# Up projections of a SwiGLU feed-forward: four grid tiles as one moving operand of 512 columns

## The chip, the core and the metric

The kernel runs on one core of a Trainium2 chip. The metric is the device time of one launch in microseconds (us); the median of three runs of the kernel before is 1928.17 us (1925.45 to 1930.57). The core has five engines that run side by side and each work through their own instructions in a fixed order: PE (TensorE: matrix products, with a separate stream of weight loads, PEld), DVE (VectorE), ACT (ScalarE), POOL (GpSimd) and SP (SyncE, here only an issuer of transfers). They wait for each other through semaphores. Matrix products are written to PSUM, which has eight banks of 128 x 512 floats.

## What is computed

A trunk of two layers over 512 latent tokens on a grid (64 wide) and 256 context tokens, with a model width of 1024. Each layer is a modulated RMSNorm, one input projection, four token mixers, an output projection with a gated residual, and then the part that matters here: a second modulated RMSNorm and a SwiGLU of hidden width 2816 with a gated residual. In the last layer the context tokens are left out of everything behind the mixers.

```
def swiglu(h, w1, w3, w2):
    return (jax.nn.silu(h @ w1) * (h @ w3)) @ w2

    for l in range(DEPTH):
        ...
        hx = rms_norm(x, norm2_g[l]) * (1.0 + scx2) + shx2
        x = x + gx2 * swiglu(hx, ffn_w1[l], ffn_w3[l], ffn_w2[l])
        if l < DEPTH - 1:
            ...
            y = y + gy2 * swiglu(hy, ffn_w1[l], ffn_w3[l], ffn_w2[l])
    return rms_norm(x, final_norm_g)
```

## The kernel before

Tokens lie in tiles of 128: tiles 0 to 3 are the grid, tiles 4 and 5 the context. Two tiles make a pair p: p = 0 and 1 for the grid, p = 2 for the context. Every large product is done with both operands split into a rounded high part and the remainder as a low part; `mm3` (L465 to L469) issues three matmuls for it, high by high (L467), high by low (L468) and low by high (L469).

The normed tokens of the second norm are made in `norm_T` (L490): per pair it transposes on PE, scales and shifts on DVE, rounds the high part on ACT (L508) and subtracts for the low part (`sub_lo`, L213). The two results of a pair are tiles of the tag `b8`, [128, 8, 256]: eight blocks k of the model width, 256 tokens each. They stay in SBUF for the whole feed-forward as `h2[p]`.

The feed-forward runs over 11 groups g of 256 hidden units. A group has

- the weights: w1 and w3 in two units of [128, 4, 256] each, w2 in two units of [128, 1024]; each is loaded into a `raw` tile (issued from ACT's queue, four buffers), rounded into `wh` on ACT (L449, five buffers) and subtracted into `wl` on DVE or POOL (L213);
- the up projections, `ffn_up(W, p)` (L1457): for both halves j of the hidden units 24 matmuls (eight k by three) into one PSUM tile `ps`, with the weights as stationary operand and 256 tokens of `h2[p]` as moving operand. For w1 ACT takes the silu into `s1` (L1464). For w3 DVE multiplies (L1466), ACT rounds the product into `gh` (L1467) and `sub_lo` puts the remainder into `gl` (L213; every third call of `sub_lo` in the whole kernel goes to POOL, the others to DVE). In the profile `s1` tiles are named P, `gh` and `gl` are named b;
- the down projection (L1490 on): for each token tile t and each half b of the output six matmuls into a PSUM tile `pg`, with `gh` and `gl` as stationary and 512 columns of w2 as moving operand: three for j = 0, three for j = 1. DVE multiplies by the gate (`nat`, L1353), POOL adds to the residual (L1355). Group 9 has no down projection of its own; it is done with group 10's.

Within a group w1 comes first for all pairs and then w3 for all pairs (pairs 2, 0, 1 in layer 0; 0, 1 in layer 1). Group 0 holds the last pair back, since its norm is still being made. In layer 0 the modulation of the next layer is computed beside this, 12 steps a group, two behind each `ffn_up`: each step loads a tile `qT` of `ada_w` (issued from ACT's queue) and multiplies and adds it on DVE (L397); at some steps PE sums over partitions (`pu`, L404) and transposes (L429) behind a copy by ACT (L426).

The text of the program gives the dependences. The order on each engine, and which PSUM bank and buffer a tile gets, are set when the program is built, by a scheduler that models durations; on the chip each engine then keeps that order.

```
                for j in range(2):
                    ps = PS("s")
                    for k in range(8):
                        mm3(ps[:, 0:256], W(k, j), (h2[p][0][:, k], h2[p][1][:, k]), k == 0, k == 7)
```

Of the kernel before, what the change touches and what calls it, by code (L numbers as in the profile page):

```python
# [7 lines left out]
F32R = mybir.dt.float32r  # L8
# [79 lines left out]
def build(tc, I, out, opts=None):  # L88
# [401 lines left out]
    def norm_T(l, which, p, blks, hT, ks, tags=("s",)):  # L490
        s = 0 if p < 2 else 1
        sh, sc = (0, 1) if which == 1 else (2, 3)
        if p not in hT:
            hT[p] = (T("b8", [P, 8, 256], F32R), T("b8", [P, 8, 256], F32R))
        hi, lo = hT[p]
        for i2, k2 in enumerate(ks):
            ps = PS(tags[i2 % len(tags)]).rearrange("p (a b) -> p a b", a=2)
            for k in range(2):
                for i in range(2):
                    pe.transpose(ps[:, k, i * P:(i + 1) * P], blks[i][k2 + k], ident)  # L500
            hf = T(HF, [P, 2, 256])
            for k in range(2):
                a, b = (modT[l][:, s, x, k2 + k:k2 + k + 1] for x in (sc, sh))
                if HFE[k]:
                    act.activation(hf[:, k], ps[:, k], AF.Identity, bias=b, scale=a)
                else:
                    dve.tensor_scalar(hf[:, k], ps[:, k], a, b, op0=ALU.mult, op1=ALU.add)
            act.activation(hi[:, k2:k2 + 2, :], hf, AF.Copy)  # L508
            sub_lo(lo[:, k2:k2 + 2, :], hf, hi[:, k2:k2 + 2, :])

    def norm_pair(l, which, p, hT):
        norm_T(l, which, p, [norm_stats(2 * p), norm_stats(2 * p + 1)], hT, range(0, 8, 2), NT_[which])
# [1 line left out]
    def hs(hT, t, k):  # L514
        hi, lo = hT[t // 2]
        o = (t % 2) * P
        return hi[:, k, o:o + P], lo[:, k, o:o + P]

    ahead = {}

# [283 lines left out]
    for l in range(LAYERS):  # L804
# [635 lines left out]
        for g in range(11):  # L1440
# [14 lines left out]
            W3 = tr_units(v3)  # L1455

            def ffn_up(W, p):  # L1457
                for j in range(2):
                    ps = PS("s")
                    for k in range(8):  # L1460
                        mm3(ps[:, 0:256], W(k, j), (h2[p][0][:, k], h2[p][1][:, k]), k == 0, k == 7)
                    sl = slice(p * 256, (p + 1) * 256)
                    if W is W1:
                        act.activation(s1[j][:, sl], ps[:, 0:256], AF.Silu)  # L1464
                        continue
                    dve.tensor_tensor(s1[j][:, sl], ps[:, 0:256], s1[j][:, sl], op=ALU.mult)  # L1466
                    act.activation(gh[j][:, sl], s1[j][:, sl], AF.Copy)  # L1467
                    sub_lo(gl[j][:, sl], s1[j][:, sl], gh[j][:, sl])

            np_ = ntile // 2  # L1470
            ps_ = [2, 0, 1] if not last else [0, 1]
            early = np_ - 1 if g == 0 else np_
            for W in (W1, W3):
                for p in ps_[:early]:
                    ffn_up(W, p)
                    steps(2)
            for p in ps_[early:]:
                ffn_up(W1, p)
# [47 lines left out]
```

## Time and profile before

| | |
|---|---|
| median of three runs | 1928.17 us (1925.45 to 1930.57) |
| the profiled execution: its time, its span | 1927.69 us, 1925.9 us |
| feed-forward of layer 0: stretch of the span, length | 550.2 to 1149.0, 598.8 us |
| feed-forward of layer 1: stretch of the span, length | 1535.6 to 1902.2, 366.6 us |
| PE busy in these two | 589.91 us and 365.02 us |
| matmuls of the up projections | 5280, each of 256 columns |
| matmuls of the down projections | 792 in layer 0, 528 in layer 1, each of 512 columns |

A span is the time from the first to the last instruction; the run's own time is 1.8 us more. A matmul's duration in the profile contains its way through the array, so that neighbours overlap; how fast PE works is read from the distance between the starts of matmuls that follow each other.

### The profile page before, as it was taken

To read this page: it belongs to the slowest core of one execution; us is meant where nothing else is said; L and a number is where in the kernel's file an instruction comes from. 1 tells how busy PE (TensorE), PEld (TensorE's weight loads), DVE (VectorE), ACT (ScalarE), POOL (GpSimd) and SP (SyncE) were. 2 spreads that over 40 slices of the span, in tenths; PEclk is the share of its full clock that TensorE was granted. 3 is DMA by queue.
4 is the path that set the end of the run, shared out by engine and by line. 5 is a ranking of instruction groups with operands and counts; after the bars stand their busy time and mean duration, and the time that the engine had idled before them with its cause. 6 is when DMAs were issued, how large, how long until landed. Compare 5 with 4: busy or idle time off the path is not lost.

```text
span 1925.9 us, 32215 instructions
## 1 busy us (share of the span) xinstructions
PE 1832.2 (95%) x12367; PEld 1596.9 (83%) x12367; DVE 1196.8 (62%) x2743; ACT 688.9 (36%) x1597; POOL 614.3 (32%) x573
## 2 busy tenths in 40 slices
PE   7899999899999999999999999899889999999997
PEld 3677776778889989999899978678778899999996
DVE  5796886777898776453334283465588854344336
ACT  3325653255542111222122233464255532222223
POOL 0211113223124553444444121111232145636442
PEclk9999999899999999999999999999999999999998
DMA  7665435453124345342222122422434143223321
GB/s 233 209 205 156 139 98 181 133 167 82 61 83 147 111 153 186 110 136 64 62 67 66 54 97 81 119 73 92 138 111 109 34 125 95 88 88 93 105 77 44
DMA packets 193572, 215.48 MB, mean 112 GB/s; under 512 B 66660, under 2 KB 141578, under 8 KB 193418
## 3 DMA queue, kind: packets, MB, share of 16 engines
q10 hardware_dynamic: 75840, 111.17, 18.3%
q1 hardware_dynamic: 117578, 102.25, 18.0%
q8 instruction: 97, 1.59, 0.3%
q14 instruction: 57, 0.47, 0.1%
HBM read 192.76 MB, written 20.63 MB: 111 GB/s over the span
## 4 chain that ended last, share of the span: by engine, by line
PE 65%; DVE 8%; issue 2%; POOL 2%; DMA 1%; ACT 1%; SPq 0%; ACTq 0%; DVEq 0%; POOLq 0%
PE ps L467 10%; PE ps L468 10%; PE ps L469 10%; PE pg L469 8%; PE pg L467 8%; PE pg L468 8%; PE po L592 2%; PE ps L626 2%; PE pt L579 2%; DVE wl L213 1%; DVE nat L1353 1%; DVE PT L397 1%; DVE P L613 1%; DVE b L1239 1%; DMA qT<-in_ada_w_dram 0%
## 5 line engine op out<-in xcount | busy, mean ns | idle before, releaser
L467 PE MATMUL ps<-b,wh 128*128 128x256 f32 x1760 | 501.9, 285 | 3.8 <-ACT P L1464 3.8
L468 PE MATMUL ps<-b,wh 128*128 128x256 f32 x1760 | 500.9, 285 | 0.0
L469 PE MATMUL ps<-b,wl 128*128 128x256 f32 x1760 | 500.3, 284 | 0.4 <-POOL wl L213 0.4
L467 PE MATMUL pg<-wh,b 128*128 128x512 f32 (+2 forms) x1128 | 441.9, 392 | 1.2 <-ACT b L508 0.9
L469 PE MATMUL pg<-wh,b 128*128 128x512 f32 (+2 forms) x1128 | 440.7, 391 | 0.6 <-POOL b L213 0.6
L468 PE MATMUL pg<-wl,b 128*128 128x512 f32 (+2 forms) x1128 | 439.6, 390 | 1.2 <-DVE rs_yn L288 0.6
L467 PEld LDWEIGHTS ps<-b,wh 128*128 128x128 f32 x1760 | 340.1, 193 | 7.1 <-ACT P L1464 4.1
L468 PEld LDWEIGHTS ps<-b,wh 128*128 128x128 f32 x1760 | 340.1, 193 | 0.8
L469 PEld LDWEIGHTS ps<-b,wl 128*128 128x128 f32 x1760 | 340.2, 193 | 0.6 <-POOL wl L213 0.6
L213 DVE TENSOR_TENSOR wl<-raw,wh 128x1024 fp32r<-128x1024 f32 (+1 forms) x130 | 200.8, 1549 | 199.0 <-ACT wh L449 197.8
L449 ACT ACTIVATE wh<-raw 128x1024 fp32r<-128x1024 f32 (+1 forms) x196 | 202.7, 1049 | 256.9 <-PE pg L469 210.4
L1355 POOL TENSOR_TENSOR b<-b,nat 128x512 f32<-128x512 f32 (+1 forms) x204 | 221.3, 1103 | 114.2 <-DVE nat L1353 81.6
L213 POOL TENSOR_TENSOR wl<-raw,wh 128x1024 fp32r<-128x1024 f32 (+1 forms) x66 | 165.9, 2514 | 265.1 <-ACT wh L449 254.3
L467 PEld LDWEIGHTS pg<-wh,b 128*128 128x128 f32 x1128 | 214.4, 190 | 38.9 <-issue 1.7
L469 PEld LDWEIGHTS pg<-wh,b 128*128 128x128 f32 x1128 | 214.2, 190 | 38.9 <-issue 3.9
L468 PEld LDWEIGHTS pg<-wl,b 128*128 128x128 f32 x1128 | 214.1, 190 | 38.1 <-DVE wl L213 1.7
L1353 DVE TENSOR_TENSOR nat<-pg,gate 128x512 f32<-128x512 f32 x240 | 162.0, 686 | 85.6 <-PE pg L469 80.2
L213 POOL TENSOR_TENSOR b<-P,b 128x256 fp32r<-128x256 f32 x36 | 28.9, 804 | 327.3 <-ACT b L1467 327.3
L1467 ACT ACTIVATE b<-P 128x256 fp32r<-128x256 f32 x110 | 45.7, 416 | 233.0 <-DVE P L1466 221.9
L1466 DVE TENSOR_TENSOR P<-ps,P 128x256 f32<-128x256 f32 x110 | 46.4, 422 | 129.6 <-PE ps L469 129.5
L1464 ACT ACTIVATE P<-ps 128x256 f32<-128x256 f32 x110 | 41.5, 383 | 213.4 <-PE ps L469 131.6
L397 DVE SCALAR_TENSOR_TENSOR PT<-qT,consts,PT 128x512 f32<-128x512 f32 x112 | 102.1, 927 | 19.3 <-DMA qT<-in_ada_w_dram 18.4
(322 smaller groups left out, 2446.5 us busy)
## 6 DMA issues: line engine op xcount, KB each, us to landing
raw<-in_ffn_w_dram ACTq DMA_DIRECT2D x132, 512.0 KB
qT<-in_ada_w_dram ACTq DMA_DIRECT2D x96, 256.0 KB
raw<-in_w_in_dram SPq DMA_DIRECT2D x40, 512.0 KB
a<-in_ada_w_dram SPq DMA_DIRECT2D x32, 256.0 KB
a<-in_ada_w_dram ACTq DMA_DIRECT2D x32, 256.0 KB
xn<-in_ada_w_dram ACTq DMA_DIRECT2D x32, 256.0 KB
raw<-in_w_out_dram SPq DMA_DIRECT2D x16, 512.0 KB
ldq<-q_d SPq DMA_DIRECT2D x40, 128.0 KB
```

The lines of the kernel that those rows point to most:

```text
L213: eng.tensor_tensor(out, full, hi.bitcast(F32), op=ALU.subtract)
L397: dve.scalar_tensor_tensor(acc[s], w, sS[:, k, s:s + 1], acc[s], op0=ALU.mult, op1=ALU.add)
L449: act.activation(hi, raw_ap, AF.Copy)
L467: pe.matmul(ps, a[0], b[0], start=first, stop=False)
L468: pe.matmul(ps, a[0], b[1], start=False, stop=False)
L469: pe.matmul(ps, a[1], b[0], start=False, stop=last)
L579: pe.transpose(ps[:, i * P:(i + 1) * P], Pm[:, (b0 + i) * P:(b0 + i + 1) * P], ident)
L1353: dve.tensor_tensor(tm, ps, gates[(0 if t < 4 else 2) + b], op=ALU.mult)
L1355: eng.tensor_tensor(ap, ap, tm[:, a:c], op=ALU.add)
L1464: act.activation(s1[j][:, sl], ps[:, 0:256], AF.Silu)
L1466: dve.tensor_tensor(s1[j][:, sl], ps[:, 0:256], s1[j][:, sl], op=ALU.mult)
L1467: act.activation(gh[j][:, sl], s1[j][:, sl], AF.Copy)
```

## The change

`norm_T` makes, for the second norm's grid pairs, four tiles of [128, 4, 512] instead of two pairs of [128, 8, 256]: two for the high and two for the low part, each with four of the blocks k and the 512 tokens of both pairs. `h2[0]` and `h2[1]` are now views of 256 columns in them, and `h2["x"]` gives all 512 columns of a block. Readers of `hT` call `hi(k)` and `lo(k)` instead of indexing a tile; the first norm's tiles and the context pair keep their form, and the SBUF used is the same.

`ffn_up(W, "x")` does the four grid tiles at once: 24 matmuls of 512 columns into one PSUM tile (a whole bank), then silu, product, rounding and remainder on 512 columns. Group 0 keeps the pairs and their order. The other ten groups of each layer do, for w1 and then for w3, the context pair (layer 0) and "x". The modulation steps come three behind each of the four calls instead of two behind each of the six.

```diff
         if p not in hT:
-            hT[p] = (T("b8", [P, 8, 256], F32R), T("b8", [P, 8, 256], F32R))
+            if which == 2 and p < 2:
+                X = [[T("b8", [P, 4, 512], F32R) for _ in range(2)] for _ in range(2)]
+                hT["x"] = [lambda k, x=x: x[k // 4][:, k % 4] for x in X]
+                for q in range(2):
+                    hT[q] = [lambda k, n=1, x=x, q=q: x[k // 4][:, k % 4:k % 4 + n, 256 * q:256 * q + 256] for x in X]
+            else:
+                X = [T("b8", [P, 8, 256], F32R) for _ in range(2)]
+                hT[p] = [lambda k, n=1, x=x: x[:, k:k + n] for x in X]
...
-            act.activation(hi[:, k2:k2 + 2, :], hf, AF.Copy)
-            sub_lo(lo[:, k2:k2 + 2, :], hf, hi[:, k2:k2 + 2, :])
+            act.activation(hi(k2, 2), hf, AF.Copy)
+            sub_lo(lo(k2, 2), hf, hi(k2, 2))
...
             def ffn_up(W, p):
+
+                sl = slice(0, 512) if p == "x" else slice(p * 256, (p + 1) * 256)
+                n = sl.stop - sl.start
                 for j in range(2):
-                    ps = PS("s")
+                    ps = PS("s")[:, 0:n]
                     for k in range(8):
-                        mm3(ps[:, 0:256], W(k, j), (h2[p][0][:, k], h2[p][1][:, k]), k == 0, k == 7)
-                    sl = slice(p * 256, (p + 1) * 256)
+                        mm3(ps, W(k, j), [x(k) if p == "x" else x(k)[:, 0] for x in h2[p]], k == 0, k == 7)
                     if W is W1:
-                        act.activation(s1[j][:, sl], ps[:, 0:256], AF.Silu)
+                        act.activation(s1[j][:, sl], ps, AF.Silu)
                         continue
-                    dve.tensor_tensor(s1[j][:, sl], ps[:, 0:256], s1[j][:, sl], op=ALU.mult)
+                    dve.tensor_tensor(s1[j][:, sl], ps, s1[j][:, sl], op=ALU.mult)
...
-            for W in (W1, W3):
-                for p in ps_[:early]:
-                    ffn_up(W, p)
-                    steps(2)
-            for p in ps_[early:]:
-                ffn_up(W1, p)
-                ffn_up(W3, p)
+            if g == 0:
+                ps_ = [2, 0, 1] if not last else [0, 1]
+                for W in (W1, W3):
+                    for p in ps_[:-1]:
+                        ffn_up(W, p)
+                        steps(2)
+                for W in (W1, W3):
+                    ffn_up(W, ps_[-1])
+            else:
+                for W in (W1, W3):
+                    for p in ([2, "x"] if not last else ["x"]):
+                        ffn_up(W, p)
+                        steps(3)
```

How the order on PE changes where the up projections of a group end and its down projection begins (here layer 1, group 5): before, the last matmul of the up projections (p = 1, j = 1) and the first nine of the down projection. Of the stationary operands, b_3569 and b_3571 are `gh` and `gl` of j = 0, b_3570 and b_3572 those of j = 1.

```order
L469 MATMUL ps_18892<-b_3315_16918,wl_18701 128x256
L467 MATMUL pg_18932<-wh_18922,b_3569_18676 128x512
L468 MATMUL pg_18932<-wl_18923,b_3569_18676 128x512
L469 MATMUL pg_18932<-wh_18922,b_3571_18678 128x512
L467 MATMUL pg_18932<-wh_18928,b_3570_18677 128x512
L468 MATMUL pg_18932<-wl_18929,b_3570_18677 128x512
L469 MATMUL pg_18932<-wh_18928,b_3572_18679 128x512
L467 MATMUL pg_18942<-wh_18922,b_3569_18676 128x512
L468 MATMUL pg_18942<-wl_18923,b_3569_18676 128x512
L469 MATMUL pg_18942<-wh_18922,b_3571_18678 128x512
```

Each output tile takes its three matmuls of j = 0 and its three of j = 1 at once. The same place on PE now; b_3513 and b_3515 are `gh` and `gl` of j = 0, b_3514 and b_3516 those of j = 1.

```order
L469 MATMUL ps_17272<-b_3248_15695,wl_17189 128x512
L467 MATMUL pg_17312<-wh_17302,b_3513_17164 128x512
L468 MATMUL pg_17312<-wl_17303,b_3513_17164 128x512
L469 MATMUL pg_17312<-wh_17302,b_3515_17166 128x512
L467 MATMUL pg_17322<-wh_17302,b_3513_17164 128x512
L468 MATMUL pg_17322<-wl_17303,b_3513_17164 128x512
L469 MATMUL pg_17322<-wh_17302,b_3515_17166 128x512
L467 MATMUL pg_17333<-wh_17302,b_3513_17164 128x512
L468 MATMUL pg_17333<-wl_17303,b_3513_17164 128x512
L467 MATMUL pg_17312<-wh_17308,b_3514_17165 128x512
L468 MATMUL pg_17312<-wl_17309,b_3514_17165 128x512
L469 MATMUL pg_17312<-wh_17308,b_3516_17167 128x512
```

Eight matmuls of j = 0, taken from three output tiles, now stand between the end of the up projections and the first use of `gh` of j = 1; two more stand before the first use of its `gl`.

On DVE in layer 0, group 1, behind the product of j = 0 of the last call: before (P_6961 is `s1` of j = 1, b_1565 its `gl`, L397 the modulation).

```order
L397 SCALAR_TENSOR_TENSOR PT_7745<-qT_7749,consts,PT_7745 128x512
L397 SCALAR_TENSOR_TENSOR PT_7746<-qT_7749,consts,PT_7746 128x512
L397 SCALAR_TENSOR_TENSOR PT_7745<-qT_7809,consts,PT_7745 128x512
L1466 TENSOR_TENSOR P_6961<-ps_7356,P_6961 128x256
L397 SCALAR_TENSOR_TENSOR PT_7746<-qT_7809,consts,PT_7746 128x512
L213 TENSOR_TENSOR b_1565_6965<-P_6961,b_1563_6963 128x256
L1353 TENSOR_TENSOR nat_7411<-pg_7404,gate_6424 128x512
```

Now:

```order
L397 SCALAR_TENSOR_TENSOR PT_7586<-qT_7653,consts,PT_7586 128x512
L397 SCALAR_TENSOR_TENSOR PT_7585<-qT_7657,consts,PT_7585 128x512
L213 TENSOR_TENSOR wl_7437<-raw_7434,wh_7436 128x1024
L1475 TENSOR_TENSOR P_6961<-ps_7242,P_6961 128x512
L397 SCALAR_TENSOR_TENSOR PT_7586<-qT_7657,consts,PT_7586 128x512
L213 TENSOR_TENSOR wl_7443<-raw_7440,wh_7442 128x1024
```

The product of j = 1 (now L1475) still stands behind modulation steps, two instead of three, and a weight remainder has moved ahead of it; its `gl` has gone to POOL.

## Rows read from the trace of the kernel before

**Rows 1.** Page: busy time of each engine; the chain that ended last.
```profile
PE 1832.2 (95%) x12367; PEld 1596.9 (83%) x12367; DVE 1196.8 (62%) x2743; ACT 688.9 (36%) x1597; POOL 614.3 (32%) x573
PE 65%; DVE 8%; issue 2%; POOL 2%; DMA 1%; ACT 1%; SPq 0%; ACTq 0%; DVEq 0%; POOLq 0%
```
**Rows 2.** Windows: the two feed-forwards; stretch, length, busy time (count), clock, DMA share.
```profile
550.20:1149.00 598.80, 589.91 (x4192) 550.78 (x4190) 346.30 (x553) 142.07 (x252) 239.36 (x215) 0.99 0.33 104
1535.60:1902.20 366.60, 365.02 (x2612) 345.72 (x2611) 163.97 (x245) 106.19 (x172) 176.14 (x146) 1.00 0.29 90
```
**Rows 3.** Timeline of PE, layer 1: start and duration; rows left out are steps alike.
```profile
1626.07 0.28 PE L469 MATMUL ps<-b,wl 128*128 128x256 f32 x1
...
1630.03 0.28 PE L469 MATMUL ps<-b,wl 128*128 128x256 f32 x1
1630.15 0.40 PE L467 MATMUL pg<-wh,b 128*128 128x512 f32 x1
...
1632.22 0.39 PE L467 MATMUL pg<-wh,b 128*128 128x512 f32 x1
...
1640.83 0.39 PE L469 MATMUL pg<-wh,b 128*128 128x512 f32 x1
1641.06 0.28 PE L467 MATMUL ps<-b,wh 128*128 128x256 f32 x1
```
**Rows 4.** Groups by form in the two feed-forwards: count, busy us, mean ns, idle before.
```profile
L467 PE MATMUL ps<-b,wh 128*128 128x256 f32 x1056 | 302.6, 287 | 3.8 <-ACT P L1464 3.8
L467 PE MATMUL ps<-b,wh 128*128 128x256 f32 x704 | 199.3, 283 | 0.0
```
**Rows 5.** Timeline of PE and DVE, layer 1, group 1, around the down projection's start.
```profile
1596.09 0.28 PE L469 MATMUL ps<-b,wl 128*128 128x256 f32 x1
1596.21 0.40 PE L467 MATMUL pg<-wh,b 128*128 128x512 f32 x1
...
1596.41 0.42 DVE L1466 TENSOR_TENSOR P<-ps,P 128x256 f32<-128x256 f32 x1 [1.54 <-PE ps L469]
1596.75 2.17 DVE L213 TENSOR_TENSOR wl<-raw,wh 128x1024 fp32r<-128x1024 f32 x1
1598.85 0.41 DVE L213 TENSOR_TENSOR b<-P,b 128x256 fp32r<-128x256 f32 x1
...
1596.87 0.42 ACT L1467 ACTIVATE b<-P 128x256 fp32r<-128x256 f32 x1 [0.56 <-DVE P L1466]
```
**Rows 6.** Groups by form, whole run, of 256 and of 512 columns.
```profile
L1466 DVE TENSOR_TENSOR P<-ps,P 128x256 f32<-128x256 f32 x110 | 46.4, 422 | 129.6 <-PE ps L469 129.5
L1353 DVE TENSOR_TENSOR nat<-pg,gate 128x512 f32<-128x512 f32 x240 | 162.0, 686 | 85.6 <-PE pg L469 80.2 <-POOL b L1355 4.6
L1467 ACT ACTIVATE b<-P 128x256 fp32r<-128x256 f32 x110 | 45.7, 416 | 233.0 <-DVE P L1466 221.9 <-DMA qT<-in_ada_w_dram 8.0 <-DMA raw<-in_ffn_w_dram 3.0
L508 ACT ACTIVATE b<-ldq 128x512 fp32r<-128x512 f32 x44 | 27.6, 629 | 39.5 <-DVE ldq L507 39.5
```
**Rows 7.** Line 213: durations min/median/max in ns of its forms.
```profile
L213 DVE TENSOR_TENSOR b<-P,b x74: 409/425/1668, 578.8 to 1892.0; 128x256 fp32r<-128x256 f32 x74
L213 POOL TENSOR_TENSOR b<-P,b x36: 727/738/1242, 570.8 to 1886.2; 128x256 fp32r<-128x256 f32 x36
L213 DVE TENSOR_TENSOR b<-ldq,b x30: 673/682/2387, 22.1 to 1551.2; 128x512 fp32r<-128x512 f32 x30
L213 POOL TENSOR_TENSOR b<-ldq,b x14: 1275/1298/2887, 30.4 to 1548.7; 128x512 fp32r<-128x512 f32 x14
```
**Rows 8.** Timeline of PE and DVE, layer 0, group 1, where its up projections end.
```profile
644.31 0.28 PE L469 MATMUL ps<-b,wl 128*128 128x256 f32 x1
...
643.48 4.22 DVE L397 SCALAR_TENSOR_TENSOR PT<-qT,consts,PT 128x512 f32<-128x512 f32 x3
647.63 0.41 DVE L1466 TENSOR_TENSOR P<-ps,P 128x256 f32<-128x256 f32 x1
```
**Rows 9.** Timeline of PE: the four waits over 1 us, with the instruction behind each.
```profile
566.64 0.30 PE L500 MATMUL pt<-consts,xn 128*128 128x128 f32 x1 [2.17 <-DVE xn L486]
...
722.79 0.58 PE L467 MATMUL ps<-b,wh 128*128 128x256 f32 x1 [3.83 <-ACT P L1464]
...
935.39 0.44 PE L429 MATMUL pu<-consts,nat 128*128 128x128 f32 x2 [2.17 <-ACT nat L426]
...
1544.28 0.30 PE L500 MATMUL pt<-consts,xn 128*128 128x128 f32 x1 [1.58 <-DVE xn L486]
```
**Rows 10.** Windows behind three of these waits (length, busy times, clock, DMA share, GB/s).
```profile
721.40:728.20 6.80, 5.41 (x25) 5.41 (x26) 3.95 (x11) 0.66 (x2) 0.49 (x1) 0.50 0.59 193
936.40:939.90 3.50, 3.50 (x19) 3.50 (x18) 0.11 (x2) 0.34 (x1) 0.00 (x0) 0.51 0.97 277
1541.50:1547.00 5.50, 3.92 (x34) 3.62 (x33) 5.05 (x24) 2.35 (x6) 0.00 (x0) 1.00 0.61 192
```

More of the change, by code (lines that the diff above doesn't have):

```diff
@@ L516, in hs @@
         o = (t % 2) * P
-        return hi[:, k, o:o + P], lo[:, k, o:o + P]
+        return hi(k)[:, 0, o:o + P], lo(k)[:, 0, o:o + P]
     ahead = {}
@@ L1457, in ffn_up @@
             def ffn_up(W, p):
+                sl = slice(0, 512) if p == "x" else slice(p * 256, (p + 1) * 256)
+                n = sl.stop - sl.start
                 for j in range(2):
-                    ps = PS("s")
+                    ps = PS("s")[:, 0:n]
                     for k in range(8):
-                        mm3(ps[:, 0:256], W(k, j), (h2[p][0][:, k], h2[p][1][:, k]), k == 0, k == 7)
-                    sl = slice(p * 256, (p + 1) * 256)
+                        mm3(ps, W(k, j), [x(k) if p == "x" else x(k)[:, 0] for x in h2[p]], k == 0, k == 7)
                     if W is W1:
-                        act.activation(s1[j][:, sl], ps[:, 0:256], AF.Silu)
+                        act.activation(s1[j][:, sl], ps, AF.Silu)
                         continue
-                    dve.tensor_tensor(s1[j][:, sl], ps[:, 0:256], s1[j][:, sl], op=ALU.mult)
+                    dve.tensor_tensor(s1[j][:, sl], ps, s1[j][:, sl], op=ALU.mult)
                     act.activation(gh[j][:, sl], s1[j][:, sl], AF.Copy)
                     sub_lo(gl[j][:, sl], s1[j][:, sl], gh[j][:, sl])
-            np_ = ntile // 2
-            ps_ = [2, 0, 1] if not last else [0, 1]
-            early = np_ - 1 if g == 0 else np_
-            for W in (W1, W3):
-                for p in ps_[:early]:
-                    ffn_up(W, p)
-                    steps(2)
-            for p in ps_[early:]:
-                ffn_up(W1, p)
-                ffn_up(W3, p)
+            if g == 0:
[11 more added lines that the diff above has]
+                        steps(3)
             for j in range(2):
```

## The prediction

> **What bounds the kernel now.** I read the page's busy times and its chain first [rows 1]: PE is busy for 95% of the span and holds 65% of the chain, and no other engine is above 62% busy. Then the windows of the two feed-forwards [rows 2]: PE is busy for 589.91 of 598.80 us in layer 0 and for 365.02 of 366.60 us in layer 1, at a granted clock of 0.99 and 1.00. So only 8.9 and 1.6 us of PE idle lie there, and a gain must come from PE's own steps. Third, the timeline of PE [rows 3]: the distance between the starts of neighbours is what a matmul costs there, not its duration. Last, the places where PE waits [rows 9], and what DVE and ACT do at the boundary between up and down projection [rows 5, 8].
>
> **What the change saves.** From 1626.07 to 1630.03 lie 33 steps of 256 columns: 3.96/33 = 0.120 us. From 1632.22 to 1640.83 lie 38 steps of 512 columns: 8.61/38 = 0.2266; over the whole down projection of a group, 10.91/48 = 0.2273 [rows 3]. Twice the columns cost 1.89 times the time: each matmul carries some 13 ns that don't depend on its columns. Two of 256 become one of 512, which saves 0.240 - 0.227 = 0.013 us (0.0127 to 0.0134). The grid's up projections of ten groups have, in each layer, two weights x two halves j x eight k x three matmuls = 96 merged ones a group; x 10 x 2 = 1920. In the built order PE's rows do fall by about that number. So 1920 x 0.013 = **25.0 us** (24.4 to 25.7). The new matmul itself is not in the trace; its nearest row is the 512-column matmul of the down projection, which has the same form (a new stationary operand each step, the moving one from SBUF, a whole PSUM bank), and I take its step.
>
> The Trainium skill ("TensorE: Matmul & The Clock Gate", section "Back-to-back issue gap") gives as the isolated step of a matmul its columns over 2.4 GHz plus some 2.5 ns, so the fixed part would be 2.5 ns instead of 13; an estimate by that page is 5 us saved instead of 25, which is a point of the last rival below. The trace shows 120 and 227 ns where that rule has 109 and 216, so the rows decide, and the sum goes by them.
>
> The rest of the edit costs nothing on PE. On ACT and DVE, two instructions on 256 columns become one on 512: on DVE 2 x 0.422 = 0.844 becomes about 0.686, on ACT 2 x 0.416 = 0.832 becomes about 0.629 [rows 6], with equal work on 128 x 512 as the nearest rows. Both engines are at 62% or less, so that is off the path. The views in `norm_T` change where a tile lies, not how much is read; the first norm and group 0 keep their order.
>
> **What it gives back: the chain behind the last up projection.** Before, `gh` and `gl` of tiles 0 and 1 were done while p = 1 was still being multiplied (48 steps x 0.12 = 5.8 us of cover), so the down projection could begin at once: its first matmul starts 0.12 behind the last of the up projections [rows 5]. Now all four tiles hang on one chain that begins with the very last matmul of j = 1. Let S be that matmul's start. It ends at S + 0.39 [rows 3]; the product takes DVE 0.686; ACT rounds in 0.629 [rows 6]; the remainder takes 0.682 on DVE or 1.298 on POOL [rows 7]; each hand-over costs 0.04 to 0.08 (DVE starts 0.04 behind PE's end, ACT 0.04 behind DVE's [rows 5]). `gh` is ready at about S + 1.85, `gl` at S + 2.5 if DVE makes it and S + 3.17 if POOL does.
>
> What covers it is the eight or more matmuls of j = 0 which the order puts first. The first use of `gh` stands 8 steps in, at S + 9 x 0.227 = S + 2.05: covered. The first use of `gl` stands at S + 2.50 (ten steps ahead of it), S + 2.72 (eleven) or, where DVE has a weight remainder in between (2.17 us [rows 5]), at S + 4.09 (seventeen), with `gl` then due near S + 3.6. By the built order there are 18 such boundaries (group 0 and the deferred group 9 have none). Twelve have `gl` on DVE or 16 steps ahead of it, and are covered if DVE is free. Six have it on POOL with ten or eleven steps of cover: layer 0, groups 4, 7 and 10, layer 1, groups 2, 5 and 8. There PE waits 3.17 - 2.50 = 0.7 (five times) and 0.5 (once): **4.0 us**. From below, 0 if POOL's work overlaps more than the rows show; from above, 18 x 0.7 = 12.6 if each chain runs as late.
>
> Layer 0, group 1 is apart. There DVE was late before: PE ended the last up projection at 644.59, and the product started at 647.63, 3.04 later, behind three modulation steps that ran for 4.22 us, waiting for `qT` [rows 8]. It cost nothing, since tiles 0 and 1 covered it. Now two modulation steps and a weight remainder stand ahead of the product, and its cover ends at S + 3.86. With the same delay `gl` comes at S + 6.2 and PE waits 2.3; with DVE free, 0. I take **1.5**, nearer to the row.
>
> **Waits that stay.** Four waits over 1 us are in rows [rows 9]. Two stand ahead of the edit, in the norm and group 0 (2.17 and 1.58), and their order is unchanged. The one of 3.83 is where ACT sits at the issue of a weight transfer until POOL's remainder, behind the residual adds of the group before, frees a buffer; the one of 2.17 at 935.39 is `pu` waiting for DVE and ACT. Behind these two the granted clock was 0.50 for 6.8 us and 0.51 for 3.5 us, and the 256-column step 0.21 instead of 0.12; behind the wait of 1.58 it was 1.00 [rows 10]. So half the time at the low level is lost: 3.83 + 3.4 + 2.17 + 1.7 = 11 us hang on these two. POOL's adds stay as many and begin a little later now; I take **+1** (gone: -10; each longer by half: +5). Small waits at the 512-column silu and product, which hold a PSUM bank longer: the whole count of 256-column matmuls with k = 0 had 3.8 us of idle time ahead of it in layer 0 and 0.0 in layer 1 [rows 4]; **+1**, from 0 to 4. The rest of PE's order moves in places in the mixers too; nothing there has a sign: 0, between -3 and +3.
>
> **The sum** against the profiled execution, 1927.69 (0.5 below the median of 1928.17): 1927.7 - 25.0 + 4.0 + 1.5 + 1 + 1 = 1910.2; on the median 1910.7. I say **1911 us**.
>
> **Rivals.**
> - *Cover everywhere.* The chain hides at all boundaries, and the two old waits in layer 0 shrink since the order around them is new. For it: twelve boundaries are covered by the rows. Against it: the adds and the `pu` steps that make those waits are unchanged. 1928 - 25 - (0 to 10) = 1893 to 1903.
> - *DVE late in layer 0.* As in group 1 [rows 8], in most of layer 0's groups the product of j = 1 stands behind modulation steps that wait for `qT`. Nine boundaries x 1 to 1.7 us in place of my 1.5 plus 2.0 for that layer: 1911 + 6 to 12 = 1917 to 1923. Against it: the other groups of layer 0 have free time on DVE (346 us busy of 599 [rows 2]).
> - *The half clock, slower.* If the nine boundaries of layer 0 make PE wait as `pu` did (2.17), and each brings the low clock for 3.5 us as there [rows 9, 10], each costs 2.2 + 1.7 = 3.9: 35 us, so 1928 - 25 + 35 + 5 = 1943. It decides from 25/9 = 2.8 us a boundary. Against it: the waits by the rows are 0.7, and the wait of 1.58 left the clock at 1.00.
> - *No gain in the step.* If a 512-column step of the up projections costs two of 256, the saving is 0 and the waits stay: 1928 + 7 = 1935; with 2.5 ns saved a merge, 1920 x 2.5 ns = 5 us, it is 1930; halfway to 25 it is 1923. Against it: the step of 0.227 is seen in every down projection.
>
> That the change does not do what it says is excluded by the built order: twenty groups with 512-column matmuls.
>
> **How the numbers follow.** Forecast, 1904 to 1917 (saved 25, given back 1 to 14): 0.62. Cover everywhere: 0.15. DVE late, 1917 to 1923: 0.13. Half clock: 0.05. No gain in the step: 0.05. About 0.3%, 5.8 us, is what a measurement can tell from no change: faster is below 1922.4, slower above 1934. Faster: 0.62 + 0.15 + 0.10, less a share of 0.06 for what no case names: 0.81. Same: 0.12, from the end of "DVE late", half of "no gain" and that share. Slower: 0.07. The range takes the forecast, most of "cover everywhere" and of "DVE late", and the ends of the unnamed mixers: 1897 to 1925.
>
> **What would show it.** In the profile after: up projections of 512 columns at steps of 0.227 in steady stretches (near 0.240: no gain). Feed-forward windows of about 598.8 - 12.5 + 5 = 591 us and 366.6 - 12.5 + 2 = 356 us. Waits of PE ahead of `pg` with `gl` of j = 1, released by POOL, 0.5 to 0.7 each, at the six boundaries named and not at the covered ones; DVE as releaser in group 1 of layer 0. A granted clock of 0.5 behind such a wait would be the half clock. The two old waits, 3.83 and 2.17, at the same places: if gone, the time falls below 1904. The prediction is wrong if PE waits at the covered boundaries, or if the difference lies outside the feed-forwards.

## The result and the profile after

The changed kernel takes 1908.78 us (median of four runs, 1906.2 to 1910.68); the kernel before took 1929.37 in the same comparison. The ratio is 0.9889, with a 95% interval from 0.987 to 0.9909: faster by 1.1%. Forecast were 1911 us and a range from 1897 to 1925. The profiled execution has a span of 1908.8 us, against 1925.9: 17.1 us less, where the medians differ by 20.6. The accounts by stage below are of the profiled executions.

The page after, busy time of each engine, beside [rows 1]:

```profile
PE 1811.7 (95%) x10447; PEld 1494.0 (78%) x10447; DVE 1187.5 (62%) x2676; ACT 672.9 (35%) x1517; POOL 605.2 (32%) x560
```

PE has 1920 matmuls fewer, and its busy time falls by 20.5 us. Since a matmul's duration contains its way through the array, the stretches and steps tell more. The two feed-forwards after, cut at the same places as [rows 2] (the second stretch ends, as there, 10.1 us ahead of the last matmul of the down projection):

```profile
552.00:1139.60 587.60, 576.04 (x3230) 494.89 (x3228) 346.91 (x515) 133.91 (x208) 231.40 (x208) 1.00 0.34 105
1524.80:1885.30 360.50, 355.07 (x1652) 296.91 (x1652) 154.21 (x210) 97.53 (x132) 175.17 (x141) 1.00 0.31 91
```

Layer 0 is shorter by 11.2 us and layer 1 by 6.1 us. The prediction had named about 591 and 356 us: layer 0 is 3 us better than that, layer 1 over 4 us worse. Elsewhere little changes: 1.8 us more ahead of the first feed-forward, where PE's order is the same, and 1.6 less in the rest.

**A table for all that follows.** For each kernel it gives, in us, the time from the first matmul of a group's up projections to the first of its down projection ("up"), and on to the next group's ("down"), added up from the timeline of PE; "between" is from the start of the last down projection of layer 0 (that of groups 9 and 10 together) to the first up projection of layer 1. Two rows with the same name are two profiles of the same program.

| | L0 up 1-10 | of it g3, g7 | L0 down 0-8 | between | L1 up g0 | L1 up 1-10 | L1 down 0-8 |
|---|---|---|---|---|---|---|---|
| before | 364.6 | 42.4, 39.7 | 147.1 | 432.1 | 26.7 | 230.3 | 98.2 |
| before (e11) | 364.6 | 42.3, 39.7 | 147.1 | 433.8 | 26.7 | 230.3 | 98.2 |
| after | 345.8 | 37.8, 35.8 | 152.9 | 432.5 | 30.8 | 217.6 | 100.6 |
| after (e8) | 347.4 | 39.4, 35.8 | 153.0 | 431.3 | 30.9 | 217.6 | 100.7 |
| e1 | 359.4 | 40.6, 36.2 | 152.5 | 429.4 | 30.9 | 230.3 | 98.5 |
| e2 | 354.9 | 39.8, 37.4 | 147.1 | 430.7 | 26.7 | 223.9 | 98.2 |
| e3 | 351.8 | 37.8, 37.6 | 152.5 | 434.4 | 26.7 | 217.6 | 98.1 |
| e4 | 350.3 | 42.2, 35.1 | 147.1 | 429.3 | 30.7 | 217.6 | 100.5 |
| e5 | 366.2 | 41.6, 39.6 | 147.1 | 429.6 | 31.2 | 230.4 | 98.2 |
| e6 | 353.7 | 42.5, 38.3 | 147.1 | 432.8 | 26.7 | 217.6 | 98.1 |
| e7 | 347.3 | 39.2, 35.8 | 147.1 | 431.1 | 26.7 | 217.6 | 98.1 |
| e9 | 343.4 | 36.5, 34.6 | 147.1 | 432.7 | 26.7 | 217.6 | 98.1 |
| e10 | 341.8 | 34.9, 34.6 | 147.1 | 437.5 | 26.9 | 217.6 | 101.6 |
| e12 | 341.8 | 34.9, 34.6 | 147.1 | 431.4 | 26.7 | 217.6 | 98.1 |

**The step and the chain.** Layer 1, group 5, timeline of PE, DVE, ACT and POOL where the up projections end, beside [rows 3, 5]:

```profile
1707.32 0.39 PE L469 MATMUL ps<-b,wl 128*128 128x512 f32 x1
...
1719.56 0.39 PE L469 MATMUL ps<-b,wl 128*128 128x512 f32 x1
1719.79 0.39 PE L467 MATMUL pg<-wh,b 128*128 128x512 f32 x1
...
1721.84 0.39 PE L468 MATMUL pg<-wl,b 128*128 128x512 f32 x1
1722.75 0.50 PE L469 MATMUL pg<-wh,b 128*128 128x512 f32 x1 [0.52 <-POOL b L213]
...
1719.99 0.69 DVE L1475 TENSOR_TENSOR P<-ps,P 128x512 f32<-128x512 f32 x1 [1.44 <-PE ps L469]
...
1720.71 0.63 ACT L1476 ACTIVATE b<-P 128x512 fp32r<-128x512 f32 x1 [3.86 <-DVE P L1475]
...
1721.42 1.28 POOL L213 TENSOR_TENSOR b<-P,b 128x512 fp32r<-128x512 f32 x1 [8.30 <-ACT b L1476]
```

From 1707.32 to 1719.56 lie 54 steps: 12.24/54 = 0.227 us, the step that was taken from the down projection. The chain, counted from the last matmul's start S = 1719.56: product at S + 0.43, rounding at S + 1.15, remainder on POOL from S + 1.86 to S + 3.14, and PE goes on at S + 3.19, 0.91 behind the matmul ahead of it instead of 0.227: a wait of 0.68, and 0.71 in the two other such groups of layer 1. The step behind it, from 1722.75 to 1723.09, takes 0.34, so that a boundary costs 0.8 us in all.

All waits of PE in the two feed-forwards after (columns: what waited, for what, us in total, times, longest), layer 0 and then layer 1:

```profile
PE pg L469 <- POOL b L213: 4.1, 4, 2.2
PE pu L429 <- ACT nat L426: 3.5, 2, 2.7
PE pt L507 <- DVE xn L486: 2.2, 1, 2.2
PE pg L469 <- DVE b L213: 1.0, 2, 0.8
PE pg L467 <- ACT b L1476: 0.6, 2, 0.3
...
PE pt L507 <- DVE xn L486: 2.6, 1, 2.6
PE pg L469 <- POOL b L213: 1.6, 3, 0.5
PE ps L469 <- DVE wl L213: 0.8, 1, 0.8
PE ps L468 <- POOL b L213: 0.5, 1, 0.5
```

The `pg` waits are the new boundary waits. They cost 5.8 us in layer 0 (down 0 to 8: 152.9 against 147.1) and 2.4 in layer 1. Behind none of them did the granted clock fall, so that the rival "half clock" has no part in them. Against before, the waits of group 0 in layer 1 are new or longer, and those of layer 0, groups 3 and 7, are smaller.

### The profile page after: what moved, and what is told of

Its sections match the earlier page's. It is cut to its first block, busy times and chain, and to the rows that moved or that the text cites. A ratio compares the mean times of both kernels' runs of the same rounds, so it can differ in the third digit from the quotient of the medians.

```text
span 1908.8 us, 28192 instructions
## 1 busy us (share of the span) xinstructions
PE 1811.7 (95%) x10447; PEld 1494.0 (78%) x10447; DVE 1187.5 (62%) x2676; ACT 672.9 (35%) x1517; POOL 605.2 (32%) x560
## 3 DMA queue, kind: packets, MB, share of 16 engines
q10 hardware_dynamic: 75840, 111.17, 18.8%
## 5 line engine op out<-in xcount | busy, mean ns | idle before, releaser
L467 PE MATMUL ps<-b,wh 128*128 128x512 f32 (+1 forms) x1120 | 388.2, 347 | 0.0
L469 PE MATMUL ps<-b,wl 128*128 128x512 f32 (+1 forms) x1120 | 386.7, 345 | 0.8 <-DVE wl L213 0.8
L468 PE MATMUL ps<-b,wh 128*128 128x512 f32 (+1 forms) x1120 | 386.9, 345 | 0.5 <-POOL b L213 0.5
L213 DVE TENSOR_TENSOR wl<-raw,wh 128x1024 fp32r<-128x1024 f32 (+1 forms) x131 | 207.4, 1592 | 174.9 <-ACT wh L449 145.3
L468 PEld LDWEIGHTS pg<-wl,b 128*128 128x128 f32 x1128 | 215.2, 191 | 39.7 <-DVE rs_yn L288 2.3
L467 PEld LDWEIGHTS ps<-b,wh 128*128 128x128 f32 x1120 | 213.5, 191 | 27.4 <-issue 2.4
L469 PEld LDWEIGHTS ps<-b,wl 128*128 128x128 f32 x1120 | 213.4, 191 | 26.0 <-DVE wl L213 1.0
L468 PEld LDWEIGHTS ps<-b,wh 128*128 128x128 f32 x1120 | 213.6, 191 | 25.5 <-POOL b L213 0.7
L1473 ACT ACTIVATE P<-ps 128x512 f32<-128x512 f32 (+1 forms) x70 | 35.4, 505 | 224.3 <-PE ps L469 128.0
L1475 DVE TENSOR_TENSOR P<-ps,P 128x512 f32<-128x512 f32 (+1 forms) x70 | 40.1, 575 | 118.9 <-PE ps L469 118.8
L1476 ACT ACTIVATE b<-P 128x512 fp32r<-128x512 f32 (+1 forms) x70 | 37.6, 538 | 195.3 <-DVE P L1475 176.0
L397 DVE SCALAR_TENSOR_TENSOR PT<-qT,consts,PT 128x512 f32<-128x512 f32 x112 | 94.0, 857 | 14.6 <-DMA qT<-in_ada_w_dram 13.3
L213 POOL TENSOR_TENSOR b<-P,b 128x512 fp32r<-128x512 f32 (+1 forms) x24 | 27.8, 1158 | 231.9 <-ACT b L1476 231.9
```

The source lines that it names most:

```text
L213: eng.tensor_tensor(out, full, hi.bitcast(F32), op=ALU.subtract)
L397: dve.scalar_tensor_tensor(acc[s], w, sS[:, k, s:s + 1], acc[s], op0=ALU.mult, op1=ALU.add)
L467: pe.matmul(ps, a[0], b[0], start=first, stop=False)
L468: pe.matmul(ps, a[0], b[1], start=False, stop=False)
L469: pe.matmul(ps, a[1], b[0], start=False, stop=last)
L1473: act.activation(s1[j][:, sl], ps, AF.Silu)
```

## The experiments

**e1: the new order without the merge.**

```diff
-                    for k in range(8):
-                        mm3(ps, W(k, j), [x(k) if p == "x" else x(k)[:, 0] for x in h2[p]], k == 0, k == 7)
+                    for q in range(2 if p == "x" else 1):
+                        for k in range(8):
+                            mm3(ps[:, 256 * q:256 * q + 256], W(k, j), [x(k)[:, 256 * q:256 * q + 256] if p == "x" else x(k)[:, 0] for x in h2[p]], k == 0, k == 7)
```

> The changed kernel in all but one thing: the four grid tiles still share one PSUM tile, one silu, one product and one chain, but each of the 1920 matmuls of 512 columns is two of 256. Theory (a fixed 13 ns a matmul): the steps are 0.120 us again and 25 us come back; the built order puts 12 to 19 instead of 8 to 16 down-projection matmuls ahead of the late operands, so some 3 us of boundary waits go: 1909 + 25 - 3 = 1931 us, between 1927 and 1936. Rival (the gain comes from the new order, which took two old waits and two stretches of half clock away, not from the step): 1912 to 1920.

1932.97 us, ratio to before 1.0021 (1.0008 to 1.0034). Timeline of PE in layer 1:

```profile
1724.90 0.28 PE L469 MATMUL ps<-b,wl 128*128 128x256 f32 x1
...
1736.42 0.28 PE L469 MATMUL ps<-b,wl 128*128 128x256 f32 x1
```

96 steps in 11.52 us: 0.120 again. L1 up 1-10 is 230.3, to a tenth that of before, and 12.7 less with the merge; the whole difference to the changed kernel is 24 us. So the gain is the step's. The boundary waits did not go as expected: in layer 0 "down" stays at 152.5, in layer 1 it falls to 98.5. Everything but the step, in the order that e1 has, costs 1.5 to 6.6 us against before (0.08 to 0.34%).

**e2: w1 alone.**

```diff
-                for W in (W1, W3):
-                    for p in ([2, "x"] if not last else ["x"]):
-                        ffn_up(W, p)
-                        steps(3)
+                for p in ([2, "x"] if not last else ["x"]):
+                    ffn_up(W1, p)
+                    steps(3)
+                for p in ([2, 0, 1] if not last else [0, 1]):
+                    ffn_up(W3, p)
+                    steps(2)
```

> 512 columns for w1 alone; w3 keeps the pairs, so gh and gl of tiles 0 and 1 are ready early as before, and every third call of sub_lo falls on the same place as before. Theory: 960 merges save 12.6 us; PE waits at no boundary to the down projection (down projections of 16.35 us in layer 0 in every group); layer 1 group 0 takes 26.7 us again: 1929 - 12.6 = 1917 if the two old waits of layer 0 stay, 1911 if they shrink as in the changed kernel. Rival (the boundary waits have to do with 512-column work on DVE and ACT at large, not with the chain behind w3): boundary waits of 5 us or more remain and the time is 1920 or above.

1913.89 us, 0.9932 (0.9905 to 0.9958), between the two values of the theory. L1 up 1-10 is 223.9, 6.4 below before for half the merges of a layer; both "down" columns are exactly those of before; group 0 of layer 1 is at 26.7. Boundary waits therefore come from the chain behind w3 alone. Layer 0 gained 3.3 us more than the steps (364.6 - 6.4 = 358.2, measured 354.9), in groups 3 and 7.

**e3: the grid's `gl` on DVE.**

```diff
-                    sub_lo(gl[j][:, sl], s1[j][:, sl], gh[j][:, sl])
+                    if p == "x":
+                        rr["lo"] += 2
+                        dve.tensor_tensor(gl[j][:, sl], s1[j][:, sl], gh[j][:, sl].bitcast(F32), op=ALU.subtract)
+                    else:
+                        sub_lo(gl[j][:, sl], s1[j][:, sl], gh[j][:, sl])
```

> The remainder gl of the grid always on DVE, never on POOL; the counter that sends every third call of sub_lo to POOL goes on as if the two calls of before had been made, so that all other calls fall where they fell before. Theory: the waits on POOL go (layer 1 groups 2, 5, 8: 2.1 us; layer 0 groups 4, 7, 10: some 3 us), and up projections of layer 1 group 0 take 26.7 us instead of 30.8, since DVE and POOL no longer have their 1024-column remainders there at once: 1909 - 9 = 1900 us, between 1897 and 1904. Rival (group 0 of layer 1 is longer for another reason, and DVE, with 14 more remainders, gets late in layer 0): 1905 to 1911, group 0 of layer 1 above 29 us.

1911.55 us, 0.9914 (0.989 to 0.9938): no gain over the changed kernel, and above the ranges of theory and rival. In layer 1 the theory is right: the boundary waits are gone (98.1) and group 0 is back at 26.7. In layer 0 PE waits again, elsewhere:

```profile
PE pu L429 <- ACT nat L426: 7.7, 3, 2.7
PE pt L507 <- DVE xn L486: 2.2, 1, 2.2
PE pg L467 <- ACT b L1476: 2.0, 7, 0.6
PE pg L469 <- DVE b L1479: 0.5, 2, 0.3
```

Down 0 to 8 stays at 152.5: PE now waits a little at nearly every boundary, mostly for `gh`, which ACT makes behind a weight rounding of 1.06 us, and a third `pu` wait appears in group 1. DVE is not what is late there, as the rival had it: in groups 4, 5 and 7 its product starts at S + 0.43, as in the undisturbed chain of layer 1.

**e4: context behind the grid for w3 in layer 0.**

```diff
-                for W in (W1, W3):
-                    for p in ([2, "x"] if not last else ["x"]):
+                for W, o in ((W1, [2, "x"]), (W3, ["x", 2])):
+                    for p in (o if not last else ["x"]):
```

> In layer 0 the w3 calls are in the order grid, context instead of context, grid, so that the 48 matmuls of the context pair (5.8 us) stand between the grid's last matmul and the down projection; layer 1 is as in the changed kernel. Theory: the 7 us of boundary waits of layer 0 go, all down projections of layer 0 take 16.35 us; layer 1 keeps its three waits of 0.7 and its 30.8 us in group 0: 1909 - 7 = 1902, between 1899 and 1906. Rival (those waits are not cover of the chain but DVE and POOL being late in layer 0 anyway): they appear at other places, 1906 to 1911.

1906.12 us, 0.9889 (0.9865 to 0.9913). Waits of PE in layer 0:

```profile
PE pu L429 <- ACT nat L426: 5.2, 2, 5.0
PE pt L507 <- DVE xn L486: 2.2, 1, 2.2
PE ps L469 <- POOL wl L213: 0.4, 1, 0.4
```

Not one boundary wait is left, and every down projection takes 16.35 us, as the theory had it; layer 1 keeps its waits. But the `pu` wait of group 3 grew from 2.7 to 5.0 and that group from 37.8 to 42.2 us; besides the wait, the granted clock behind it was 0.68 over 7.2 us, against 1.00 in the first profile of the changed kernel. The time is 2.7 us below the changed kernel's, not 7, and lies at the low end of the rival's range.

**e5: the kernel before with the counter moved by one.**

```diff
         for _ in ada_todo:
             pass
+        if l == 0:
+            rr["lo"] += 1
```

> The kernel before with one thing added: the counter that sends every third call of sub_lo to POOL is advanced by one at the end of layer 0, as the 20 calls that the change leaves out advance it (112 calls instead of 132 in that feed-forward, which is one place on in threes). Theory (the 4.1 us lost in layer 1, group 0, come from which remainders fall on POOL): its up projections take 30.8 us instead of 26.7, the other groups 23.03 as before, and the time is 1929 + 4 = 1933 us, give or take 3 for the mixers of layer 1, whose calls shift as well. Rival (the 4.1 us come from the new form of the normed tiles or of the group's code): 26.7 us, 1929.

1931.25 us, 1.0008 (0.9997 to 1.002), so the total is not told from before; group 0 of layer 1, however, takes 31.2 us, and the stretch between the feed-forwards happens to be 2.4 shorter. The cause of the 4.1 us is shown: which remainders fall on POOL. Timelines of DVE, POOL and PE there: the changed kernel, then e3, with the same work in another allotment.

```profile
1524.55 2.84 DVE L213 TENSOR_TENSOR wl<-raw,wh 128x1024 fp32r<-128x1024 f32 x1
1527.31 2.88 DVE L1362 TENSOR_TENSOR b<-b,nat 128x512 f32<-128x512 f32 x1
...
1523.66 2.64 POOL L213 TENSOR_TENSOR wl<-raw,wh 128x1024 fp32r<-128x1024 f32 x1 [2.58 <-ACT wh L449]
1526.99 2.65 POOL L213 TENSOR_TENSOR wl<-raw,wh 128x1024 fp32r<-128x1024 f32 x1 [0.69 <-ACT wh L449]
...
1527.44 0.39 PE L469 MATMUL ps<-b,wl 128*128 128x256 f32 x1 [0.77 <-DVE wl L213]
1535.05 0.33 PE L507 MATMUL pt<-consts,xn 128*128 128x128 f32 x1 [2.56 <-DVE xn L486]
```

```profile
1528.08 0.69 DVE L1362 TENSOR_TENSOR b<-b,nat 128x512 f32<-128x512 f32 x1
1528.68 1.22 DVE L213 TENSOR_TENSOR wl<-raw,wh 128x1024 fp32r<-128x1024 f32 x1
...
1528.79 3.38 POOL L213 TENSOR_TENSOR wl<-raw,wh 128x1024 fp32r<-128x1024 f32 x1 [2.37 <-ACT wh L449]
...
1537.41 0.30 PE L507 MATMUL pt<-consts,xn 128*128 128x128 f32 x1 [1.58 <-DVE xn L486]
```

In the changed kernel the DVE remainder (1.22 in e3) begins while POOL works and ends 1.1 behind POOL's end at 1526.30; the add behind it (0.69 in e3) meets POOL's second remainder and ends 0.55 behind that. DVE loses nearly 4 us, and the norm for which PE waits stands behind it.

**e6 and e7: both remedies, and remainders of w1 and w3 off POOL.** e6 has e4's order, e3's branch in layer 1 alone, and the counter moved one further for each `gl` of the grid in layer 0. e7 adds for layer 0, from group 1 on, `dve` as the engine of `split_unit` for w1 and w3.

> Grid before context for w3 in layer 0; gl of the grid on DVE in layer 1; the counter advanced so that all other remainders fall where they fell before the change. Theory: no boundary waits in either layer (layer 0 down projections 16.35 us, layer 1 10.91), group 0 of layer 1 at 26.7: against the changed kernel -7.1 -2.1 -4.1 = -13, and 3 to 5 us given back at the two waits on the modulation's transposes (pu) in layer 0, which stay and may be longer: 1909 - 13 + 4 = 1900, between 1896 and 1904. Rival (what is saved at boundaries is lost again at the pu waits, since POOL's adds set that time): 1904 to 1910.

1901.77 us, 0.9855 (0.9836 to 0.9875). Boundary waits are gone in both layers, group 0 is at 26.7, and groups 3 and 7 of layer 0 take 42.5 and 38.3: as expected, the old waits swallow a part.

> As the run before, and in layer 0 from group 1 on the remainders of w1 and w3 always on DVE. Theory on the two pu waits (in groups 3 and 7 ACT sits at the issue of a weight transfer whose buffer a remainder on POOL, queued behind 18 residual adds, still reads; so pu's copy on ACT is late): the waits go, groups 3 and 7 take 35 us or less for their up projections instead of 38 to 42, and it is 3 to 7 us faster than the run before: 1894, between 1890 and 1899. Rival (ACT or DVE is late there for another reason, the modulation's own transfers qT or the remainder on DVE that POOL's adds hold up): the waits stay, 1898 to 1905.

1896.45 us, 0.9827 (0.9811 to 0.9842): 5.3 us faster than e6. The `pu` waits shrank (groups 3 and 7: 39.2 and 35.8) but did not go; the time lies in the theory's range, its mechanism is half confirmed.

**e8 and e11: second profiles.**

> The changed kernel a second time, for a second profile. Theory (what the order and the engine of each step decide, repeats; what transfers decide, does not): the waits of 0.7 us at the boundaries of layer 1 and layer 0 group 4, and 30.8 us in layer 1 group 0, within 0.1; the two pu waits (2.84 and 1.05 in the first profile) may differ by 1 us or more. Rival (the pu waits are of the order too): they come back within 0.3. Time 1909, between 1905 and 1913.

> The kernel before a second time, for a second profile. Theory (the waits of layer 0 are of the order on the engines): 3.83 and 2.17 us come back at the same places within 0.3; whether the granted clock falls to 0.5 behind them may differ, 0 to 5 us. Rival (they are of the transfers' timing): they differ by over 1 us.

1909.68 us, 0.9894 (0.9878 to 0.991), and 1927.61 for one run of before. In e8 the waits at `pu` are 3.6 us in all, as in the first profile (3.5), and before has 42.3 and 39.7 us in groups 3 and 7 again. These waits belong to the order on the engines; the rival of e8 was right. What does vary is the granted clock behind them: in the changed kernel it stayed at 1.00 in the first profile and was 0.76 over the 7.2 us behind the wait in e8, which makes group 3 longer by 1.6 us. The `pg` waits behind DVE and `qT` vary too (group 1: 0.83 and 1.51 us of idle time).

**e9, e10, e12: what holds ACT.** e9 is e7 with the remainders of w2 in layer 0 on DVE too. e10 is e7 with SP instead of ACT as issuer of all feed-forward weights. e12 is e9 with SP as issuer for layer 0 from group 2 on.

```diff
-                    Q["wf"].dma_start(raw, v[:, 4 * u:4 * u + 4, c0:c0 + 256])
+                    (sp if g > 1 and not last else Q["wf"]).dma_start(raw, v[:, 4 * u:4 * u + 4, c0:c0 + 256])
```

The same stands at the load of w2.

> As e7, and the remainders of w2 in layer 0 (from group 1 on) on DVE too, so that POOL has only residual adds and gl there. Theory (the last remainder on POOL, 2.35 us behind the adds, still sets when ACT passes the weight transfer's issue in group 3): the pu waits of 2.7 and 1.1 us shrink by 1 to 2 us each, 1894, between 1890 and 1897. Rival (the adds themselves, or DVE held up by them, set it): the waits stay and it is 1895 to 1900.

> As e7, but the weights of the feed-forward are issued from SP's queue instead of ACT's, so that a transfer whose buffer is not yet free stops SP and not ACT. Theory (ACT is late at the pu copies only because it stands at that issue): no pu wait above 0.5 us in groups 3 and 7, which take 34.5 us or less for their up projections (33.9 without waits, and matmuls of the modulation among them); 1890, between 1886 and 1895. Rival (pu's sums come late themselves, from DVE and from qT): the waits stay above 1 us; 1894 to 1900.

> As e9, with SP's queue for the feed-forward weights of layer 0 from group 2 on, and ACT's for the rest, so that neither the loads around group 0 nor those of layer 1, with which e10 lost what it had won, change their queue. Theory: group 3 of layer 0 goes from 36.5 to 34.9 us for its up projections, nothing else changes: 1.5 us faster than e9, 1892, between 1888 and 1895. Rival (e10's loss in the mixers of layer 1 comes from the loads of layer 0's last groups on SP): the stretch between the two feed-forwards grows by some 5 us again and the time is 1896 or more.

e9: 1893.23 us, 0.9804 (0.9773 to 0.9835), as its theory had it; one `pu` wait, of 1.4 us, is left, and group 3 takes 36.5. e10: 1904.05, 0.9873 (0.9844 to 0.9901): no `pu` wait at all in layer 0, groups 3 and 7 at 34.9 and 34.6, yet 6.5 us more between the feed-forwards than e7 and 3.5 more in layer 1's down projections, so that the time misses both of its ranges. e12: 1890.43, 0.979 (0.9769 to 0.9811): group 3 at 34.9 as in e10, without that loss, which therefore hangs on the loads around group 0 and of layer 1; why these suffer on SP's queue was not followed further. In the total e12 is not told from e9. e12 is 2.1% faster than before and beats both kernels.

The rows that e10 explains are these, layer 0, group 3: POOL, DVE, ACT and PE in the changed kernel, and ACT in e10 (ACTq is ACT's issue of transfers).

```profile
714.05 2.04 POOL L1362 TENSOR_TENSOR b<-b,nat 128x512 f32<-128x512 f32 x2
...
718.65 0.76 POOL L1362 TENSOR_TENSOR ldr<-ldr,nat 128x256 f32<-128x256 f32 x1
719.34 2.42 POOL L213 TENSOR_TENSOR wl<-raw,wh 128x1024 fp32r<-128x1024 f32 x1
...
714.70 0.69 DVE L1360 TENSOR_TENSOR nat<-pg,gate 128x512 f32<-128x512 f32 x1 [0.67 <-PE pg L469]
715.31 7.53 DVE L213 TENSOR_TENSOR wl<-raw,wh 128x1024 fp32r<-128x1024 f32 x1
...
722.87 0.39 ACTq L1454 DMA_DIRECT2D raw<-in_ffn_w_dram  x1
723.35 0.38 ACT L1473 ACTIVATE P<-ps 128x256 f32<-128x256 f32 x1 [7.32 <-DVE PT L395]
...
724.57 0.44 PE L429 MATMUL pu<-consts,nat 128*128 128x128 f32 x2 [2.67 <-ACT nat L426]
```

```profile
720.96 0.38 ACT L1473 ACTIVATE P<-ps 128x256 f32<-128x256 f32 x1 [2.55 <-PE ps L469]
721.50 0.38 ACT L426 ACTIVATE nat<-pu 128x256 f32<-128x256 f32 x1 [0.16 <-PE pu L404]
```

In the changed kernel ACT's issue of a weight transfer comes at 722.87, right behind the end, at 722.84, of DVE's remainder, which began at 715.31 and ended 1.1 behind POOL's row of adds and remainder (721.76); the silu and the copy for `pu` follow. In e10 ACT waits for PE alone. So ACT's stand at the issue makes this wait, and the end of POOL's 18 adds and its remainder sets how long ACT stands, as the prediction said of before. That also tells why e4 and e6 won nothing there. From the start of group 2's down projection to the end of group 3's up projections it is 58.7 us in before (16.35 + 42.37), 55.6 and 57.2 in the two profiles after, 58.6 in e4 and 58.8 in e6, though the last two have no boundary wait. PE comes early in them, but POOL's remainder ends no earlier: 25.8 us behind the start of that down projection in before, 25.1 and 25.0 after, 27.6 in e4 and 27.1 in e6. Most of the rest is the granted clock. Over the 7.2 us behind the wait it was 0.62 in before, 1.00 and 0.76 after, 0.68 in e4 and 0.59 in e6; 7.2 us times what it lacks to 1 gives, as an estimate, lost times of 2.7, 0, 1.7, 2.3 and 3.0 us, and without them all five lie between 55.5 and 56.3.

## Why the prediction was right

- **The saving, 25.0 us:** right. Measured are 12.7 us in layer 1 (230.3 - 217.6) and, by e1, 24 us in all. The step of 0.227 was rightly read off the down projection. The 2.5 ns a matmul that the Trainium skill ("TensorE: Matmul & The Clock Gate", "Back-to-back issue gap") gives for the isolated step is not what these streams show: twice 0.120 against 0.227.
- **The chain on POOL, 0.7 a boundary:** right where the prediction had put it in layer 1, groups 2, 5 and 8 (0.68 to 0.71), and in layer 0, groups 4 and 7 (0.71 and 0.69). In group 10 the wait is 2.3 instead of 0.5. Timeline of POOL and PE there:

```profile
1093.54 2.37 POOL L213 TENSOR_TENSOR wl<-raw,wh 128x1024 fp32r<-128x1024 f32 x1 [12.99 <-ACT wh L449]
1095.87 1.26 POOL L213 TENSOR_TENSOR b<-P,b 128x512 fp32r<-128x512 f32 x1
...
1097.19 0.50 PE L469 MATMUL pg<-wh,b 128*128 128x512 f32 x1 [2.15 <-POOL b L213]
```

  The step that failed here took POOL for free; a weight remainder stands right ahead of `gl`.
- **"Covered if DVE is free":** in groups 2, 3 and 6 of layer 0 PE waited at boundaries that the prediction had called covered, for 1.2, 0.8 and 0.5 us; by its own sign this part of it was wrong. In group 2 a modulation step on DVE stood between product and `gl`, and what made it long was a remainder on POOL:

```profile
697.85 2.39 POOL L213 TENSOR_TENSOR wl<-raw,wh 128x1024 fp32r<-128x1024 f32 x1 [3.43 <-ACT wh L449]
...
698.19 2.60 DVE L397 SCALAR_TENSOR_TENSOR PT<-qT,consts,PT 128x512 f32<-128x512 f32 x1
700.71 0.68 DVE L213 TENSOR_TENSOR b<-P,b 128x512 fp32r<-128x512 f32 x1
...
701.45 0.97 PE L469 MATMUL pg<-wh,b 128*128 128x512 f32 x3 [0.80 <-DVE b L213]
```

  The step, 0.75 us long elsewhere, ended 0.55 behind the remainder. In group 3 such a step of 2.96 us beside POOL's remainder stood ahead of the product. In group 6 DVE was free (product at S + 0.43), but ACT had a weight to round before `gh`, whose own rounding began at S + 2.51 instead of S + 1.15:

```profile
906.95 1.06 ACT L449 ACTIVATE wh<-raw 128x1024 fp32r<-128x1024 f32 x1 [3.00 <-POOL wl L213]
```

  So the rival "DVE late in layer 0" came true in two of its nine groups: 2.0 us in place of its 6 to 12.
- **"Waiting for `qT`":** the prediction read this out of the 4.22 us of three modulation steps in [rows 8], and it is not so. The last of the three began at 644.81 and took 2.90 us, beside this remainder on POOL in the kernel before, and ended 0.55 behind it:

```profile
644.21 2.95 POOL L213 TENSOR_TENSOR wl<-raw,wh 128x1024 fp32r<-128x1024 f32 x1 [4.59 <-ACT wh L449]
```

  A true wait for `qT` stands in the trace as idle time ahead of the step. Group 1, taken at 1.5, cost 1.0 and, in e8, 1.7. There DVE had waited for `qT` a little earlier, for 0.87 and 1.70 us, and its product came at S + 1.18 and S + 2.01; the releaser of PE was POOL with `gl`, not DVE as the prediction said.
- **"Waits that stay", +1:** wrong sign. Groups 3 and 7 give 6.1 us back in the first profile of after (364.6 - 345.8 = 18.8, less 12.7 of steps) and 4.5 in the second. The idle time fell from 3.83 and 2.17 to 2.67 and 0.88 us, and the half clock behind them was missing in the first profile. In before it cost some 2.7 and 1.7 us: of the 6.8 us at the low level behind the first wait PE worked for 5.41 only [rows 10], so that the prediction's 3.4 was too much. Whether the clock falls there is not settled by the program: two profiles of the same kernel differ in it. The shrinking of these waits is the half of the rival "cover everywhere" that came true. The prediction had added the later start of POOL's adds to this wait; but part of what PE would wait for them it now waits at the boundary ahead of them.
- **"Their order is unchanged"** of the wait in layer 1, group 0: this step failed, and cost 4.1 us. The text of group 0 is unchanged, but the counter in `sub_lo` reaches it in another phase, since ten groups make two calls fewer each. PE's order alone had been looked at there, not POOL's. Some 2.5 us of it are waits, two new ones and 1.0 more ahead of the norm's transposes; the rest is the granted clock, which was 0.50 for 3.41 us behind that wait, now 2.56, where the 1.58 of before had left it at 1.00.
- **Silu and product on 512 columns, +1:** 0. No matmul with k = 0 waited for a bank.
- **The sum:** forecast were -25 + 7.5 = -17.5. In the two profiled spans it is -25.4 for the steps (2 x 12.7), -6.1 for the old waits, +5.8 at the boundaries of layer 0 and +2.5 in the down projection of its groups 9 and 10, +2.4 in layer 1, +4.1 in its group 0, and -0.4 elsewhere: -17.1, which is 1908.8 - 1925.9. The old waits (7 us better than forecast), the boundaries (5 us worse) and group 0 of layer 1 (4 us worse) nearly cancelled. The saving was understood; that the total came so close was luck.

## What to carry to other kernels

Where PE is busy all the time and its matmuls have a cost that doesn't depend on their columns, merging moving operands pays that cost times the number of merges, and a stream of the wider form elsewhere in the trace gives the step in advance. What it takes away is the cover of the first halves: the consumer behind has to be given other work for the length of the chain (here another pair's matmuls, e4), or the chain has to be kept off the slow engine (e3 in layer 1). When calls are dealt to engines by a counter, any change in the number of calls deals all the later ones anew; compare every engine's order, far behind the change too.

## What the runs showed of the hardware

A DVE instruction with two inputs in SBUF could stand still while POOL ran its own on SBUF. Of the 112 modulation steps beside layer 0's feed-forward, 19 in before and 11 after took more than 1.1 us instead of 0.75, and every one of them ended 0.55 us behind the end of an instruction on POOL. It need not be for one instruction only: a remainder of 1.2 us took 2.84 us beside one POOL instruction and 7.53 us beside a row of five adds and a remainder, ending 1.1 us behind the last of them. The Trainium skill ("SBUF — State Buffer", "SBUF: two separate sides") calls the port pair of the two engines an exclusive lock, held for a whole instruction; these rows agree, and show that the other engine's next instruction can take it again before the waiting one gets it. It does not always: in e4 the same remainder got through beside the same row of adds, and POOL's add, 0.73 elsewhere, waited for it. What decides this was not tested.

```profile
711.02 1.60 DVE L213 TENSOR_TENSOR wl<-raw,wh 128x1024 fp32r<-128x1024 f32 x1
...
711.49 1.72 POOL L1362 TENSOR_TENSOR ldr<-ldr,nat 128x256 f32<-128x256 f32 x1
```

A DVE instruction with one input in PSUM was not lengthened: the gate's product (`nat<-pg,gate`, 0.69 us) at 714.70 ran beside POOL's adds from 714.05 on.
